# Hybrid encoder trunk on one core: rms factors spread by a matrix product of ones with a diagonal, negated logits, and half-swapping copies on ScalarE

## The chip, the core and the metric

The program runs on one NeuronCore of a Trainium2 chip. The core has TensorE (PE in the profile; its weight loads are PEld), VectorE (DVE), ScalarE (ACT), GpSimd (POOL) and SyncE (SP, which here only issues DMAs). The metric is the device time of one execution in microseconds (us); lower is better.

## What is computed

The input x is 512 tokens by 1024 features in float32. Two layers follow each other, each with an RMS norm, one input projection whose columns feed three groups, and one output projection that is added to x. The reference, cut down:

```python
def rmsnorm(x, w):
    y = x * rsqrt(mean(x * x, axis=-1, keepdims=True) + EPS)
    return y * w

def hybrid_layer(x, ...):                       # called twice
    h = rmsnorm(x, norm_w)
    aq, ak, av, ag, bq, bk, bv, bg, cu, cg = split(h @ w_in)
    # A: 4 heads, two softmax maps each, logits = q.k / 8 + bias[q - k]
    o_a = rmsnorm((softmax(l0) - lam * softmax(l1)) @ v) * silu(ag)
    # B: 4 heads of two-way retention, rotary q and k, chunks of 128
    o_b = headnorm(forward + backward) * silu(bg)
    # C: pooling over windows of 2, 4, 8, 16, minus the token, then a linear map
    o_c = pool_mix(cu) * silu(cg)
    return x + concat(o_a, o_b, o_c) @ w_out

out = rmsnorm(layer1(layer0(x)), final_norm_w)
```

## The kernel before

**Precision.** Every matrix product works on operands that are split in a high and a low part of type float32r. `split` does it: ScalarE writes the high part (a CAST), VectorE subtracts it from the source and writes the low part. `mm3` then issues three matmuls where the mathematics has one.

**Weights.** They come in 95 blocks of 512 KB and two half blocks, called granules. Each is loaded by a DMA into `wraw` (2 buffers), split by ScalarE into `wh` and by VectorE into `wl` (5 buffers each). A `wraw` buffer is free again when both have read it, so VectorE's subtraction decides when the next load may be issued.

**The order.** The kernel is first recorded as a list of operations. `Recorder.schedule` plays the five engines forward with a table of costs (`cost`, `LATENCY`) and priorities (`HIGH`) and takes at each step the operation that can start first. What comes out is a fixed order for each engine; every engine then executes its own list strictly in that order. All DMAs are issued by SP, in one list: a DMA that waits holds up all DMAs behind it. The strings in `ORDERS` say in which order the units of a layer (projections, heads, pooling groups) are recorded.

**The first layer's start.** `first_values` multiplies the transposed x by the weights before the RMS factors are known, with the norm weights alone applied. The factor of each token (1/rms) comes later, from `square` on ScalarE and a power on GpSimd, and stands in four columns `rc` (128 partitions by 4, inside the tile `edge`). The values use it per partition. All other projections of the first layer have tokens along the free axis, so there the factor is needed as a tile `rb`, 128 partitions by 512, each partition holding all 512 factors. The unit `R` of the string `START` makes it by two DMAs, through a row in DRAM:

```python
row = nc.tile("dram", "row", [S], 4, F32)
nc.sync.dma_start(row.rearrange("(t p) -> p t", t=NT), self.rc)
nc.sync.dma_start(self.rb, row.partition_broadcast(P))
```

The users of `rb` are the rotary tables `cos` and `sin` (multiplied by it once), `scaled_T` and `c_pool`.

**Half-swapping copies.** `stack_halves` lays the queries and keys of two maps or heads into partitions 0 to 63 and 64 to 127. For the keys (`dup` is true) high and low part are also copied to the other half of the partitions, 64 by 1024 elements each time, 24 times in all. `b_qk` does the same with the retention states `sx`, 64 by 512 elements, 8 times. Both are VectorE copies before (`DUP = nc.vector`); the trace calls them CAST, since the output type is float32r; `sx` lives in a tile named `T`.

**Softmax.** In `a_head` one VectorE instruction (CUSTOM_DVE_ANT_0 in the trace) adds the bias to the logits and takes each row's maximum into the tile `sm`; a second one, 128 by 1, turns the sign; ScalarE then computes the exponential with that as its bias. This happens 64 times.

Of the kernel before, what the change touches and what calls it, by code (L numbers as in the profile page):

```python
# [369 lines left out]
def record(ins: dict, out: bass.AP):  # L370
# [3 lines left out]
    def sb(tag, shape, bufs=1, dt=F32, name=None):  # L374
        return nc.tile("sb", tag, shape, bufs, dt)
# [16 lines left out]
    def soft():  # L392
        return sb("soft", [P, S], 4)
# [20 lines left out]
    nc.vector.memset(neghalf, -0.5)  # L414
    nc.scalar.copy(sb("st", [P, 4], 4), neghalf)
    ident = sb("ident", [P, P])


    granules = [(i, shape) for i, (_, _, _, shape) in enumerate(weight_granules())]
# [19 lines left out]
    def take(n):  # L439
# [2 lines left out]
        while len(wt) < min(i + WBUFS, len(granules)):  # L442
            emit_granule()
        return wt[i:i + n]

    DUP = nc.vector


    def split(dh, dl, src):
# [68 lines left out]
    def stack_halves(dst, slots, src, scale, dup):  # L518


        for m in range(2):
            a, b = slice(64 * m, 64 * m + 64), slice(64 - 64 * m, P - 64 * m)
            s0 = slots + (2 * m if dup else m)
            hi = dst[a, s0, :]
            lo = dst[a, s0 + 1, :] if dup else dst[b, s0, :]
            if scale == 1.0:
                split(hi, lo, src[a, :])
            else:
                nc.scalar.activation(hi, src[a, :], AF.Copy, scale=scale)
                nc.vector.scalar_tensor_tensor(lo, src[a, :], scale, hi.bitcast(F32), op0=ALU.mult, op1=ALU.subtract)  # L530
            if dup:
                DUP.tensor_copy(dst[b, s0:s0 + 2, :], dst[a, s0:s0 + 2, :].bitcast(F32))

    def headnorm(ov, scale, g):

# [96 lines left out]
    def bias_tables():  # L632

        oh, ohr = ttile(), ttile(dt=F32R)
        rb = soft()[0:32, 0:4]
        rbs = sb("rbs", [64, 4], 1, F32R)
        nc.sync.dma_start(rb, ins["rel_bias"])
        nc.sync.dma_start(oh[0:64, :], ins["c_onehot"])
        nc.scalar.copy(ohr[0:64, :], oh[0:64, :])
        split(rbs[0:32, :], rbs[32:64, :], rb)  # L640
        gsb = ttile()
        for i in range(2):
            ps = lgp()
            nc.tensor.matmul(ps[0:4, :], rbs, ohr[0:64, HALF[i]], start=True, stop=True)
            nc.vector.tensor_copy(gsb[0:4, HALF[i]], ps[0:4, :])
        nc.sync.dma_start(gdram, gsb[0:4, :])


        dl = soft()
        nc.sync.dma_start(dl, ins["diff_lambda"].rearrange("l a d -> (l a d)").partition_broadcast(P))  # L650
        dv = dl.rearrange("p (l a b d) -> p l a b d", l=2, a=2, b=2)
        pr = soft()[:, 0:256].rearrange("p (l a d) -> p l a d", l=2, a=2)
        nc.vector.tensor_tensor(pr, dv[:, :, :, 0, :], dv[:, :, :, 1, :], op=ALU.mult)
        ls = cols[:, 12:16]
        nc.vector.tensor_reduce(ls, pr.rearrange("p l a d -> p (l a) d"), axis=AX.X, op=ALU.add)
        nc.scalar.activation(ls, ls, AF.Exp)
        for l in range(DEPTH):
            lam_init = 0.8 - 0.6 * math.exp(-0.3 * l)
            nc.vector.tensor_tensor(lam_t[l], ls[:, 2 * l:2 * l + 1], ls[:, 2 * l + 1:2 * l + 2], op=ALU.subtract)
            nc.vector.tensor_scalar(lam_t[l], lam_t[l], lam_init, None, op0=ALU.add)  # L660
# [18 lines left out]
    class Layer:  # L679
# [18 lines left out]
        def first_values(self):  # L698

            self.vh, self.vl = sb("vh", [P, NT, 512], 1, F32R), sb("vl", [P, NT, 512], 1, F32R)  # L700
            self.rb, self.rc = sb("rb", [P, S]), edge[:, 28:32]

            dummy = sb("soft", [P, S], 4, mybir.dt.bfloat16)
            nc.vector.memset(dummy, 0.0)
            warm = tpp()
            for _ in range(WARM):
                nc.tensor.matmul(warm[:, 0:256], dummy[:, 0:P], dummy[:, 0:256], start=True, stop=True)
            banks = [lgp(), lgp(), ovp(), pj()]
            for u in START.split():
                i = int(u[1:] or 0)  # L710
                if u[0] == "k":
                    xw = ttile()
                    nc.sync.dma_start(xw[:, 0:S + 4], ins["xT_w"][i * P:(i + 1) * P, :])
                    raw, w = xw[:, 0:S], xw[:, S:S + 1]
                    nc.scalar.activation(self.hh[:, i, :], raw, AF.Copy, scale=w)
                    nc.vector.scalar_tensor_tensor(self.hl[:, i, :], raw, w, self.hh[:, i, :].bitcast(F32), op0=ALU.mult, op1=ALU.subtract)
                    if i % 2 == 0:
                        emit_granule(2 if i < FINE else 1)
                    wh, wl = wt[i // 2]
                    for t in range(NT):  # L720
                        ts = slice(t * P, (t + 1) * P)
                        mm3(banks[t], self.hh[:, i, ts], self.hl[:, i, ts], wh[:, i % 2, :], wl[:, i % 2, :], i == 0, i == KD - 1)
                elif u[0] == "x":
                    load_x(i)
                    for half in range(2):
                        square(i, half, soft())
                    nc.vector.tensor_copy(self.rc[:, i:i + 1], stats[i][:, 2:3])
                elif u[0] == "I":
                    nc.sync.dma_start(ident, ins["c_ident"])
                elif u[0] == "R":  # L730
                    row = nc.tile("dram", "row", [S], 4, F32)
                    nc.sync.dma_start(row.rearrange("(t p) -> p t", t=NT), self.rc)
                    nc.sync.dma_start(self.rb, row.partition_broadcast(P))
                else:
                    for t in range(NT):
                        self.store_values(t, banks[t])
            wstate[0] = 4
# [51 lines left out]
        def b_qk(self, pr):  # L789
# [30 lines left out]
            for hd in range(2):  # L820
                a, b = slice(64 * hd, 64 * hd + 64), slice(64 - 64 * hd, P - 64 * hd)
                src = sv[a, :, hd * P:(hd + 1) * P]
                nc.scalar.activation(sx[a, hd, 0, :, :], src, AF.Copy, scale=0.125)
                nc.vector.scalar_tensor_tensor(sx[a, hd, 1, :, :], src, 0.125, sx[a, hd, 0, :, :].bitcast(F32),
                                               op0=ALU.mult, op1=ALU.subtract)
                nc.vector.tensor_copy(sx[b, hd, :, :, :], sx[a, hd, :, :, :].bitcast(F32))
            self.qk["B", pr] = t, qx, sx

        def b_head(self, h):
# [24 lines left out]

        def a_qk(self, h):
            t = sb("qk", [P, 6, S], 2, F32R)
            stack_halves(t, 0, *self.scaled_T(proj_T(self.hh, self.hl), 0.125), False)
            stack_halves(t, 2, *self.scaled_T(proj_T(self.hh, self.hl)), True)
            self.qk["A", h] = t

        def a_head(self, h):
# [3 lines left out]
            for half in range(2):  # L865
                ah, al = ttile([P, NT, 256], F32R), ttile([P, NT, 256], F32R)
                for i2 in range(2):
                    i = half * 2 + i2
                    st = sb("sm", [P, 8], 4)
                    e = []  # L870
                    for mp in range(2):
                        lg = lgp()
                        mm_stacked(lg, qk, mp, slice(i * P, (i + 1) * P))
                        s = soft()
                        nc.vector.tensor_tensor_reduce(s, lg, toep_tile(bt, i), scale=1.0, scalar=-3e38,
                                                       op0=ALU.add, op1=ALU.max, accum_out=st[:, mp:mp + 1])
                        nc.vector.tensor_scalar(st[:, 2 + mp:3 + mp], st[:, mp:mp + 1], -1.0, None, op0=ALU.mult)
                        nc.scalar.activation(s, s, AF.Exp, bias=st[:, 2 + mp:3 + mp], accum_out=st[:, 4 + mp:5 + mp])
                        e.append(s)
                    nc.vector.reciprocal(st[:, 6:8], st[:, 4:6])  # L880
                    nc.vector.tensor_tensor(st[:, 7:8], st[:, 7:8], lam_t[self.l], op=ALU.mult)
                    nc.scalar.activation(e[1], e[1], AF.Copy, scale=st[:, 7:8])
                    nc.vector.scalar_tensor_tensor(e[0], e[0], st[:, 6:7], e[1], op0=ALU.mult, op1=ALU.subtract)
                    tv = transpose4(e[0])
                    split(ah[:, :, i2 * P:(i2 + 1) * P], al[:, :, i2 * P:(i2 + 1) * P], tv)
                for kt in range(NT):
                    mm3(ov[:, half * 256:(half + 1) * 256], self.vh[:, kt, h * P:(h + 1) * P],
                        self.vl[:, kt, h * P:(h + 1) * P], ah[:, kt, :], al[:, kt, :], kt == 0, kt == NT - 1)
# [226 lines left out]
```

## Time and profile before

| what | value |
|---|---|
| median of 3 runs | 682.93 us (681.54 to 682.99) |
| the profiled execution, own time | 682.16 us |
| its span, first to last instruction | 680.4 us |
| PE busy | 660.3 us (97%) |
| DVE busy | 500.3 us (74%) |
| ACT busy | 354.0 us (52%) |
| POOL busy | 30.3 us (4%) |
[...]

The profile shows one execution. Busy time of PE is modelled: a 128x512 matmul is shown with some 0.40 us, while the next one starts 0.23 us after it, so they overlap, and lost time of PE is better read from the starts. A wait that is shown for an engine costs something only where that engine, or who waits for it, is the one that sets the end.

### The profile page before, as it was taken

What the parts mean: (1) busy time and instruction counts of PE and PEld (TensorE: products, weight loads), DVE (VectorE), ACT (ScalarE), POOL (GpSimd) and SP (SyncE); (2) the same over time, 40 slices, a digit from 0 to 9 for tenths busy, and PEclk for the clock granted to TensorE, in tenths of its full rate; (3) what the DMA queues carried; (4) which work ended last, traced back from release to release, by engine and by line L of the source; (5) the groups of instructions that cost most, each with busy time, mean ns of one, the idle gap of its engine ahead of it and who ended that gap; (6) DMA issues with size and microseconds to landing.
All of it is one profiled execution on the core that took longest, in us unless ns stands there. A gap on an engine that the chain in (4) does not pass through costs nothing. (4 is left out here: it accounts for less than half of the span.)

```text
span 680.4 us, 8912 instructions
## 1 busy us (share of the span) xinstructions
PE 660.3 (97%) x3171; PEld 541.3 (80%) x3171; DVE 500.3 (74%) x954; ACT 354.0 (52%) x701; POOL 30.3 (4%) x51
## 2 busy tenths in 40 slices
PE   9959999999999999999999999899999999999996
PEld 6747887888788888887888888688888887888785
DVE  4558988787787998976574778767568857887733
ACT  6524683534376866553443766344437765665321
POOL 0000000000000000001010000000000000000011
PEclk9969999999999999999999999999999999999999
DMA  8436434422225223243312423532331143124302
GB/s 309 163 123 187 141 93 125 124 93 78 87 61 171 77 91 104 72 116 95 107 63 78 139 68 85 139 109 73 104 118 59 62 137 107 61 92 97 92 31 93
DMA packets 29973, 71.86 MB, mean 106 GB/s; under 512 B 6004, under 2 KB 10260, under 8 KB 29928
## 3 DMA queue, kind: packets, MB, share of 16 engines
q1 hardware_dynamic: 29928, 71.29, 34.4%
q8 instruction: 25, 0.41, 0.3%
q14 instruction: 20, 0.16, 0.1%
HBM read 69.09 MB, written 2.18 MB: 105 GB/s over the span
## 5 line engine op out<-in xcount | busy, mean ns | idle before, releaser
L1047 PE MATMUL pj<-hh,wh 128*128 128x512 f32 x448 | 178.5, 400 | 8.7 <-ACT wh L1047 7.2
L1047 PE MATMUL pj<-hl,wh 128*128 128x512 f32 x448 | 177.8, 397 | 0.0
L1047 PE MATMUL pj<-hh,wl 128*128 128x512 f32 x448 | 177.2, 397 | 0.0
L1047 ACT CAST wh<-wraw 128x1024 fp32r<-128x1024 f32 (+1 forms) x97 | 100.8, 1039 | 108.5 <-PE pj L1047 73.9
L1047 DVE TENSOR_TENSOR wl<-wraw,wh 128x1024 fp32r<-128x1024 f32 (+1 forms) x97 | 117.3, 1209 | 28.5 <-ACT wh L1047 28.0
L1047 PEld LDWEIGHTS pj<-hh,wh 128*128 128x128 f32 x448 | 84.9, 190 | 27.8 <-ACT wh L1047 7.6
L1047 PEld LDWEIGHTS pj<-hh,wl 128*128 128x128 f32 x448 | 84.8, 189 | 18.7
L1047 PEld LDWEIGHTS pj<-hl,wh 128*128 128x128 f32 x448 | 84.8, 189 | 17.8
L1047 PE MATMUL pj<-wh,mAC 128*128 128x512 f32 (+1 forms) x264 | 87.9, 392 | 0.4 <-ACT mAC L1047 0.2
L1047 ACT ACTIVATE soft<-soft,sm 128x512 f32<-128x512 f32 x96 | 67.8, 718 | 33.7 <-DVE sm L1047 33.2
L1047 DVE TENSOR_TENSOR x<-x,pj 128x512 f32<-128x512 f32 (+1 forms) x65 | 43.5, 675 | 23.3 <-PE pj L1047 22.7
L1047 PEld LDWEIGHTS pj<-wh,mAC 128*128 128x128 f32 x264 | 48.9, 188 | 11.4 <-ACT mAC L1047 0.6
L1047 PE MATMUL lg<-qk 128*128 128x512 f32 (+1 forms) x192 | 51.3, 361 | 1.6 <-DVE soft L1047 1.6
L1047 PE MATMUL pj<-wl,mAC 128*128 128x512 f32 (+1 forms) x132 | 51.4, 389 | 0.0
L1047 POOL TENSOR_TENSOR st<-st,neghalf 128x4 f32<-128x4 f32 (+1 forms) x28 | 25.1, 897 | 477.4 <-DVE st L1047 379.3
L1047 DVE CUSTOM_DVE_ANT_0 soft<-lg,wide 128x512 f32<-128x512 f32 x64 | 43.2, 685 | 2.0 <-PE tp L1047 0.4
L1047 PE MATMUL pj<-wh,mB 128*128 128x512 f32 (+1 forms) x136 | 44.5, 383 | 0.0
L1047 PE MATMUL pj<-wh,hl 128*128 128x512 f32 x104 | 41.4, 398 | 0.0
L1047 PE MATMUL pj<-wh,hh 128*128 128x512 f32 x104 | 41.3, 397 | 0.0
L1047 PE MATMUL pj<-wl,hh 128*128 128x512 f32 x104 | 41.2, 396 | 0.0
L1047 PEld LDWEIGHTS lg<-qk 128*128 128x128 f32 x192 | 32.5, 188 | 9.6 <-DVE soft L1047 2.6
L1047 PE MATMUL ov<-T,vh 128*128 128x256 f32 x192 | 39.1, 283 | 0.4 <-DVE og L1047 0.3
(151 smaller groups left out, 948.7 us busy)
## 6 DMA issues: line engine op xcount, KB each, us to landing
wraw<-in_wg SPq DMA_DIRECT2D x95, 512.0 KB, 3.9
hn<-row SPq DMA_DIRECT2D x16, 256.0 KB, 3.9
wide<-gd SPq DMA_DIRECT2D x8, 448.0 KB, 3.8
T<-in_xT_w SPq DMA_DIRECT2D x8, 258.0 KB, 4.6
x<-in_x SPq DMA_DIRECT2D x8, 256.0 KB, 4.8
wide<-dd SPq DMA_DIRECT2D x8, 256.0 KB, 4.8
out<-T SPq DMA_DIRECT2D x8, 256.0 KB, 2.1
qd<-dd SPq DMA_DIRECT2D x8, 128.0 KB
```

The costliest lines, as they stand in the source:

```text
L1047: op.inst = getattr(getattr(tc.nc, name), method)(*[real(a) for a in op.args], **{k: real(v) for k, v in op.kw.items()})
```

## The change

Four things are altered.

1. **The factors' tile.** The two DMAs of unit `R` go. VectorE multiplies the identity matrix by each of the four columns of `rc` (a diagonal in each 128 by 128 block of `dg`), `split` makes `dh` and `dl` of it, and two matmuls with a stationary matrix of ones (128 by 128, exact in float32r) add up each column over the partitions. The sum, the factor of that column's token, arrives in all 128 partitions of a PSUM bank; ScalarE copies it to `rb`. The ones are made at the program's start, in the buffers of the tiles `T` and `u`.
2. **Negated logits.** The queries are scaled by -0.125, the bias table is written with its sign turned, the custom instruction takes the minimum, and the exponential runs with `scale=-1.0`. The instruction that turned the sign, 64 times, goes.
3. **Keys' copies** of `stack_halves` run on ScalarE.
4. **States' copies** of `b_qk` run on ScalarE.

```diff
@@ record @@
     ident = sb("ident", [P, P])
+    ones = sb("u", [P, UW], 1, F32R)[:, 0:P]
+    onesf = sb("T", [P, 1024], 4)[:, 0:P]
+    nc.vector.memset(onesf, 1.0)
+    nc.vector.tensor_copy(ones, onesf)
...
-    DUP = nc.vector
...
@@ stack_halves @@
             if dup:
-                DUP.tensor_copy(dst[b, s0:s0 + 2, :], dst[a, s0:s0 + 2, :].bitcast(F32))
+                nc.scalar.copy(dst[b, s0:s0 + 2, :], dst[a, s0:s0 + 2, :].bitcast(F32))
...
@@ bias_tables @@
-            nc.vector.tensor_copy(gsb[0:4, HALF[i]], ps[0:4, :])
+            nc.vector.tensor_scalar(gsb[0:4, HALF[i]], ps[0:4, :], -1.0, None, op0=ALU.mult)
...
@@ first_values, unit R @@
-                    row = nc.tile("dram", "row", [S], 4, F32)
-                    nc.sync.dma_start(row.rearrange("(t p) -> p t", t=NT), self.rc)
-                    nc.sync.dma_start(self.rb, row.partition_broadcast(P))
+                    dg, dh, dl = soft(), sb("soft", [P, S], 4, F32R), sb("soft", [P, S], 4, F32R)
+                    for t in range(NT):
+                        nc.vector.tensor_scalar(dg[:, t * P:(t + 1) * P], ident, self.rc[:, t:t + 1], None, op0=ALU.mult)
+                    split(dh, dl, dg)
+                    ps = tpp()
+                    nc.tensor.matmul(ps, ones, dh, start=True, stop=False)
+                    nc.tensor.matmul(ps, ones, dl, start=False, stop=True)
+                    nc.scalar.copy(self.rb, ps)
...
@@ b_qk @@
-                nc.vector.tensor_copy(sx[b, hd, :, :, :], sx[a, hd, :, :, :].bitcast(F32))
+                nc.scalar.copy(sx[b, hd, :, :, :], sx[a, hd, :, :, :].bitcast(F32))
...
@@ a_qk @@
-            stack_halves(t, 0, *self.scaled_T(proj_T(self.hh, self.hl), 0.125), False)
+            stack_halves(t, 0, *self.scaled_T(proj_T(self.hh, self.hl), -0.125), False)
...
@@ a_head @@
-                        nc.vector.tensor_tensor_reduce(s, lg, toep_tile(bt, i), scale=1.0, scalar=-3e38,
-                                                       op0=ALU.add, op1=ALU.max, accum_out=st[:, mp:mp + 1])
-                        nc.vector.tensor_scalar(st[:, 2 + mp:3 + mp], st[:, mp:mp + 1], -1.0, None, op0=ALU.mult)
-                        nc.scalar.activation(s, s, AF.Exp, bias=st[:, 2 + mp:3 + mp], accum_out=st[:, 4 + mp:5 + mp])
+                        nc.vector.tensor_tensor_reduce(s, lg, toep_tile(bt, i), scale=1.0, scalar=3e38,
+                                                       op0=ALU.add, op1=ALU.min, accum_out=st[:, mp:mp + 1])
+                        nc.scalar.activation(s, s, AF.Exp, bias=st[:, mp:mp + 1], scale=-1.0, accum_out=st[:, 4 + mp:5 + mp])
```

Since the planner plays all engines forward, the order of the whole program is made anew. At three places it matters for what follows. A row names the line, the operation, what it writes and reads with the buffers' numbers, and the shape; numbers differ between the two programs.

SP's list of DMAs before, from the last two x tiles on (`row` and `rb` are the two DMAs of unit `R`; `wraw` are weight granules):

```order
L1047 DMA x_0_253<-in_x 128x512
L1047 DMA wraw_262<-in_wg 128x1024
L1047 DMA wraw_276<-in_wg 128x1024
L1047 DMA soft_287<-in_decay 8x2
L1047 DMA row_319<-edge_112 128x4x1
L1047 DMA rb_339<-row_319 128x512
L1047 DMA wraw_348<-in_wg 128x1024
L1047 DMA wraw_397<-in_wg 128x1024
```

And SP's list at the same place now:

```order
L1055 DMA x_0_254<-in_x 128x512
L1055 DMA wraw_263<-in_wg 128x1024
L1055 DMA wraw_277<-in_wg 128x1024
L1055 DMA soft_312<-in_decay 8x2
L1055 DMA wraw_345<-in_wg 128x1024
L1055 DMA wraw_413<-in_wg 128x1024
L1055 DMA wraw_423<-in_wg 128x1024
```

The two DMAs are gone, and the load of the next granule (`wraw_348` before, `wraw_345` now) stands directly behind the small load of the decays.

ACT's list before, from the cast of the first gate's weights on (`vh` are the values, `wh` the weights' high parts; `wh_381` is the granule that `wraw_348` above loads):

```order
L1047 CAST wh_315<-wraw_262 128x1024
L1047 ACTIVATE vh_325<-lg_119,edge_112 128x512
L1047 ACTIVATE vh_325<-lg_121,edge_112 128x512
L1047 ACTIVATE vh_325<-ov_125,edge_112 128x512
L1047 ACTIVATE soft_287<-soft_287 8x2
L1047 ACTIVATE vh_325<-pj_128,edge_112 128x512
L1047 CAST wh_356<-wraw_276 128x1024
L1047 CAST wh_381<-wraw_348 128x1024
```

And now (`soft_329` is `dh`, `rb_377` the factors' tile out of the PSUM bank `tp_342`; `wh_387` answers to `wh_381`):

```order
L1055 CAST wh_320<-wraw_263 128x1024
L1055 CAST soft_329<-soft_289 128x512
L1055 ACTIVATE vh_335<-lg_120,edge_113 128x512
L1055 ACTIVATE vh_335<-lg_122,edge_113 128x512
L1055 ACTIVATE soft_312<-soft_312 8x2
L1055 ACTIVATE vh_335<-ov_126,edge_113 128x512
L1055 ACTIVATE vh_335<-pj_129,edge_113 128x512
L1055 CAST wh_365<-wraw_277 128x1024
L1055 COPY rb_377<-tp_342 128x512
L1055 CAST wh_387<-wraw_345 128x1024
```

Two instructions are new, the cast of `dh` ahead of the values and the copy of `rb` between two weight casts; the other eight stand in the order of before.

PE's list before, from the last matmuls of the values on (`pj_337` is the projection of the first gate):

```order
L1047 MATMUL pj_128<-wl_266,hh_104 128x512
L1047 MATMUL pj_128<-wh_257,hl_110 128x512
L1047 MATMUL pj_337<-hh_104,wh_315 128x512
L1047 MATMUL pj_337<-hl_110,wh_315 128x512
L1047 MATMUL pj_337<-hh_104,wl_327 128x512
```

And now:

```order
L1055 MATMUL pj_129<-wl_267,hh_105 128x512
L1055 MATMUL pj_129<-wh_258,hl_111 128x512
L1055 MATMUL tp_342<-soft_329,u_75 128x512
L1055 MATMUL pj_348<-hh_105,wh_320 128x512
L1055 MATMUL pj_348<-hl_111,wh_320 128x512
L1055 MATMUL pj_348<-hh_105,wl_331 128x512
L1055 MATMUL pj_348<-hh_105,wh_320 128x512
L1055 MATMUL pj_348<-hl_111,wh_320 128x512
L1055 MATMUL tp_342<-soft_350,u_75 128x512
L1055 MATMUL pj_348<-hh_105,wl_331 128x512
```

The two products with the ones (`u_75`) are set ahead of and between the first gate's matmuls (`pj_348`), which followed the values directly before.

## Rows read from the trace of the kernel before

**Rows 1.** The page: busy times, and TensorE's granted clock in 40 slices.

```profile
PE 660.3 (97%) x3171; PEld 541.3 (80%) x3171; DVE 500.3 (74%) x954; ACT 354.0 (52%) x701; POOL 30.3 (4%) x51
...
PEclk9969999999999999999999999999999999999999
```

**Rows 2.** Waits of PE: who waited for whom, us in total, times, longest.

```profile
PE pj L1047 <- ACT wh L1047: 7.2, 1, 7.2
PE lg L1047 <- DVE soft L1047: 1.6, 2, 1.3
PE pj L1047 <- DVE gate L1047: 1.5, 1, 1.5
PE tp L1047 <- DVE soft L1047: 1.2, 1, 1.2
PE lg L1047 <- ACT T L1047: 1.0, 1, 1.0
```

**Rows 3.** Timeline of PE, 27 to 47 us: start, duration, instruction, idle before.

```profile
27.88 0.40 PE L1047 MATMUL pj<-hh,wh 128*128 128x512 f32 x1
...
33.71 0.39 PE L1047 MATMUL pj<-hl,wh 128*128 128x512 f32 x1
41.32 0.80 PE L1047 MATMUL pj<-hh,wh 128*128 128x512 f32 x1 [7.22 <-ACT wh L1047]
...
46.56 0.40 PE L1047 MATMUL pj<-hh,wh 128*128 128x512 f32 x1
```

**Rows 4.** One window: stretch, its length, busy of five engines, PEclk, DMA share, GB/s.

```profile
41.32:46.56 5.24, 5.24 (x12) 4.17 (x13) 4.86 (x20) 1.68 (x2) 0.00 (x0) 0.51 0.64 191
```

**Rows 5.** Timelines of ACT, SP and DVE around that wait.

```profile
40.22 1.04 ACT L1047 CAST wh<-wraw 128x1024 fp32r<-128x1024 f32 x1 [10.52 <-DMA wraw<-in_wg]
...
25.06 0.39 SPq L1047 DMA_DIRECT2D row<-edge  x1
35.30 0.34 SPq L1047 DMA_DIRECT2D rb<-row  x1
35.74 7.45 SPq L1047 DMA_DIRECT2D wraw<-in_wg  x3
...
25.50 1.23 DVE L1047 TENSOR_TENSOR wl<-wraw,wh 128x1024 fp32r<-128x1024 f32 x1 [0.47 <-ACT wh L1047]
...
39.07 0.69 DVE L1047 TENSOR_TENSOR cos<-cos,rb 128x512 f32<-128x512 f32 x1 [8.56 <-DMA rb<-row]
...
41.63 1.21 DVE L1047 TENSOR_TENSOR wl<-wraw,wh 128x1024 fp32r<-128x1024 f32 x1
```

**Rows 6.** Timelines of ACT and DVE: what the new steps stand beside.

```profile
28.07 0.69 ACT L1047 ACTIVATE vh<-pj,edge 128x512 fp32r<-128x512 f32 x1
28.66 1.04 ACT L1047 CAST wh<-wraw 128x1024 fp32r<-128x1024 f32 x1
...
55.78 1.05 ACT L1047 ACTIVATE T<-T 8x1024 f32<-8x1024 f32 x1
...
0.89 0.27 DVE L1047 MEMSET soft<- 128x256 uint32 x1
```

**Rows 7.** Groups of instructions by shape: count, busy us, mean ns, idle before.

```profile
L1047 DVE CAST qk<-qk 64x1024 fp32r<-64x1024 f32 x24 | 16.5, 689 | 0.7
L1047 DVE TENSOR_SCALAR sm<-sm 128x1 f32<-128x1 f32 x64 | 8.7, 146 | 0.0
L1047 DVE CAST T<-T 64x512 fp32r<-64x512 f32 x8 | 3.4, 422 | 0.3
...
L1047 ACT CAST qk<-soft 64x512 fp32r<-64x512 f32 x32 | 19.8, 618 | 7.4 <-DVE soft L1047 3.5 <-PE lg L1047 3.4
L1047 ACT COPY hn<-ov 128x512 f32<-128x512 f32 x16 | 9.4, 586 | 16.1 <-DVE og L1047 11.0 <-PE ov L1047 4.0 <-DVE mAC L1047 0.9
...
L1047 ACT CAST T<-T 64x1024 fp32r<-64x1024 f32 x1 | 1.1, 1054 | 0.2 <-PE ov L1047 0.2
```

**Rows 8.** One window (columns as in rows 4), where retention heads are prepared.

```profile
70.00:80.00 10.00, 10.00 (x46) 8.07 (x45) 8.71 (x12) 7.90 (x12) 0.00 (x0) 1.00 0.40 136
```

## The prediction

> **What bounds the kernel now.** I read the busy times first, then PE's waits, then the timelines around the longest wait. PE is busy for 660.3 of 680.4 us, DVE for 500.3 and ACT for 354.0 [rows 1]. So PE sets the end, and work on DVE or ACT costs time only where PE waits for it. PE's list of waits [rows 2] has one large entry: 7.2 us, once, on a weight cast of ACT. The next ones are 1.6 us and less.
>
> That wait begins at 34.1 us and ends at 41.32 [rows 3]. [...] The whole loss comes from starts of matmuls. From 27.88 to 33.71 there are 25 steps, (33.71 - 27.88) / 25 = 0.233 us each. From 33.71 to 46.56 there are 13 steps (the one across the wait, and twelve behind it), which at that pace need 3.03 us; they took 12.85. The loss is **9.82 us**: some 7.4 of idleness and 2.4 of half clock.
>
> The cause stands in the rows of the other engines [rows 5]. The awaited cast began at 40.22, having waited for its granule. SP issued that load at 35.74, right behind `rb<-row`, issued at 35.30, which had to wait for `row<-edge`, issued at 25.06. The write of 512 single numbers to DRAM took 10 us, and SP's list stood still for it. DVE stood still as well: `cos` times `rb` began at 39.07 after 8.56 us of idleness, and the subtractions that make `wl` are queued behind it. Would SP have been free, the load could have been issued when its buffer was: a subtraction on the earlier granule began at 25.50 and took 1.23, so at 26.8.
>
> **The change part by part.**
>
> *The DMAs of unit R.* Both go; the load of the next granule moves up behind a small load. What must then be in time?
> - Issue 26.8, plus the landing as it was seen (35.74 to 40.22, 4.48 us [rows 5]): 31.3. Cast 1.04: 32.3.
> - PE ends the values at 27.88, has two products more (0.47) and the first gate's 24 matmuls (5.59): 33.94. It wants that cast two matmuls later, at 34.4. Reserve 2.1 us.
>
> *What takes their place.* Four multiplications of 128x128 on DVE: between 0.146 (128x1) and 0.422 (64x512) each [rows 7]; I take 0.2. They stand where DVE idled, ahead of the subtraction at 25.50. Cast of `dh`: 0.62 (the cast of 512 elements a partition [rows 7]). Subtraction for `dl`: 0.69 (as `cos` [rows 5]), from 26.73 on, so done by some 27.8 with three tiny steps between; PE wants it after the sixth matmul, at 29.3. The copy of `rb`: ACT's last values cast was at 28.07 [rows 6]; the `dh` cast moves it to 28.7, it takes 0.69, a weight cast 1.04, the copy 0.59 [rows 7]: `rb` is there at 31.0 instead of 39.07. On the path stand only the two products: **+0.47 us**.
>
> *DVE behind rb.* From `cos` to the beginning of the second subtraction it took 41.63 - 39.07 = 2.56 us [rows 5]; one values' low part (0.7, the size of `cos`) now stands between. So the first `wl` is ready at 31.0 + 2.56 + 0.7 = 34.3; PE wants it after four matmuls, at 34.87. Reserve 0.6 us: tight, and taken as no wait. Behind it 48 matmuls run until 45.1.
>
> *The next tight place* is the decay tables' exponential on ACT, behind a chain of small steps on DVE; the cast of a later granule is queued behind it. From `cos` to the end of the exponential it took 56.83 - 39.07 = 17.8 us [rows 5, 6]. From 31.0 that gives 48.8, and 49.8 with the cast; PE wants that cast 16 matmuls behind 45.1, at 48.8. So the bound from above is a wait of 1.0 us. From below it is none, since in the trace of before this chain was also held by PE itself, which now is earlier. I take none and keep 1.0 for the range.
>
> *The half clock.* With no long idleness there, nothing in the trace gives it a reason: in all other slices the digit is 9, with PE at work [rows 1]. Those 2.4 us go too.
>
> *The start.* A memset of 128x128 stands ahead of the memset on which PE's first matmuls wait: half of a 128x256 one, 0.27 / 2 = 0.14 [rows 6]. Between 0 (PE's first real matmul waits for a DMA) and 0.14; I take **0.1**.
>
> *Copies to ACT.* DVE loses 24 x 0.689 and 8 x 0.422, 19.9 us. ACT gains 24 x 1.054 and 8 x 0.618, 30.2 us [rows 7]. Where they lie, ACT is busy 7.9 and DVE 8.7 of 10 us [rows 8]; a pair of heads moves two copies of each kind, so 3.3 us more for ACT and 2.2 less for DVE, spread over some 20 us. ACT has the room. Cost on the path: bounded from above by all of ACT's surplus, 10.3 us (the slower rival), from below by a gain, since waits of 1.6, 1.5 and 1.2 us are ended by DVE [rows 2]. I take **0**: the keys' cast itself ends none of the listed waits.
>
> [...] ACT needs 1054 ns for 64x1024 where DVE needs 689 [rows 7], 365 ns more a copy. [...]
>
> *The sign.* 64 instructions of 146 ns, 9.3 us with the time counted singly, 8.7 as busy time [rows 7], each between a maximum and its exponential. PE has other matmuls to run in the attention heads, so on the path **0**; from below a part of the DVE waits above.
>
> **Sum.** -9.82 + 0.47 + 0.1 = -9.25 us. Against the profiled execution (682.16 us, 680.4 of them span) this gives 672.9; that execution lies 0.77 below the median of 682.93, so for the median **673.7 us**.
>
> **The rivals.**
> - *As summed:* 673.7; with the small terms' bounds 671.9 to 675.5.
> - *The wait comes back in part.* `rb` or the decay chain is 1.5 us later than reckoned: PE then waits 0.9 at the first tight place and, counting both, 2.5 at the second. 673.7 + 2.5 = 676.2. For it: the reserves of 0.6 and -1.0. Against: PE's own wait is contained in the 17.8 us.
> - *More is won.* The lighter DVE ends the waits that it caused: 1.6 + 1.5 + 1.2 = 4.3 [rows 2]; two thirds of them, 2.9, give 670.8. Against: the waits on banks and on attention weights can hang on a DMA or on the new order as well.
> - *The wait was hidden anyway.* If the granule's load is late for another reason (its landing takes twice the 4.48 us in the traffic there), the cast ends at 36.8 instead of 32.3, PE waits 2.4, and its clock might fall again (2.4): 678.5. Against: the 4.48 us were seen with the load of `rb` right ahead [rows 5], which is gone.
> - *Slower.* ACT works strictly in order, so a copy of 1.05 us holds up what is queued behind it, the values and the casts for PE. If all 32 copies pass on their surplus of 10.3 us to PE, the sum is -9.25 + 10.3 = +1.0: 684.0. It turns at 9.25 / 32 = 0.29 us of PE for each copy; to be slower by over 0.2% it takes 0.33. Against: ACT is idle for half of the span [rows 1].
> - *The change doesn't do what it says:* excluded here as far as the order goes; the two DMAs are gone and the load has moved up.
>
> **How the numbers follow.** Chances: as summed 0.66, back in part 0.13, more won 0.12, hidden anyway 0.05, slower 0.04. A measurement of this kernel can tell about 0.2% (1.4 us) from no change. Faster by more: all but the last, less 0.01 that several small losses meet: 0.95. Within: 0.02. Slower: 0.03. The range of 8 in 10 takes the first case whole and the nearer parts of the second and third: 670.9 to 676.8.
>
> **What would show it.** Right: no wait of PE over 1 us between 28 and 60 us, `wraw` issued near 27 us, `rb` copied near 31, the clock digit of the third slice at 9. DVE some 27 us less busy, ACT some 31 more. Wrong: PE waits on `wl` near 34.9 or on a `wh` cast near 49; ACT's copies among the instructions that end waits of PE in the heads; or new waits of several us in the second layer, where only the order has changed.

## The result, and the profile after

The changed kernel takes 672.37 us in the median of 4 runs (671.47 to 673.67), where the kernel before took 682.83 (681.54 to 682.99). The ratio is 0.9852, 95% interval 0.9829 to 0.9876, which is 8.5 to 11.7 us less; the forecast was 9.25 less, 673.7. The profiled execution of after took 673.67 us, 671.9 of them span. It is the slowest of its four, so the two profiles lie 8.49 us apart and not 10.46.

Busy times, clock digits and PE's complete list of waits, for after (for before [rows 1, 2]):

```profile
PE 658.4 (98%) x3173; PEld 539.2 (80%) x3173; DVE 478.6 (71%) x865; ACT 385.5 (57%) x735; POOL 30.1 (4%) x51
...
PEclk9999999999999999999999999999999999999999
```

```profile
PE tp L1055 <- DVE soft L1055: 2.2, 2, 1.4
PE pj L1055 <- DVE gate L1055: 1.4, 1, 1.4
PE lg L1055 <- DVE soft L1055: 1.2, 2, 0.8
PE tp L1055 <- ACT hn L1055: 1.1, 2, 0.9
PE pj L1055 <- ACT soft L1055: 0.6, 1, 0.6
PE pj L1055 <- DVE vl L1055: 0.5, 1, 0.5
PE pj L1055 <- ACT u L1055: 0.2, 1, 0.2
```

The wait of 7.2 us on the weight cast is gone, and the 6 in the clock digits with it. What remains are single waits of 1.4 us and less, none of them between 28 and 60 us. The timelines of ACT, SP, DVE and PE at the place of the old wait (start, duration, instruction, idle before):

```profile
25.47 0.63 ACT L1055 CAST soft<-soft 128x512 fp32r<-128x512 f32 x1
...
29.50 0.58 ACT L1055 COPY rb<-tp 128x512 f32<-128x512 f32 x1
29.99 1.05 ACT L1055 CAST wh<-wraw 128x1024 fp32r<-128x1024 f32 x1
...
44.75 1.06 ACT L1055 ACTIVATE T<-T 8x1024 f32<-8x1024 f32 x1 [2.11 <-DVE T L1055]
45.72 1.03 ACT L1055 CAST wh<-wraw 128x1024 fp32r<-128x1024 f32 x1
```

```profile
26.70 8.27 SPq L1055 DMA_DIRECT2D wraw<-in_wg  x3
```

```profile
30.12 0.69 DVE L1055 TENSOR_TENSOR cos<-cos,rb 128x512 f32<-128x512 f32 x1 [0.35 <-ACT rb L1055]
...
32.20 1.21 DVE L1055 TENSOR_TENSOR wl<-wraw,wh 128x1024 fp32r<-128x1024 f32 x1
```

```profile
27.69 0.39 PE L1055 MATMUL tp<-soft,u 128*128 128x512 f32 x1
27.93 0.39 PE L1055 MATMUL pj<-hh,wh 128*128 128x512 f32 x1
29.07 0.39 PE L1055 MATMUL tp<-soft,u 128*128 128x512 f32 x1
...
33.96 0.39 PE L1055 MATMUL pj<-hl,wh 128*128 128x512 f32 x1
...
36.96 0.40 PE L1055 MATMUL pj<-hh,wh 128*128 128x512 f32 x1
```

The load that was issued at 35.74 [rows 5] is now issued at 26.70, its cast begins at 29.99, and `cos` at 30.12 instead of 39.07. From 27.69 (the first product with the ones, right behind the values) to 36.96 PE makes 40 steps in 9.27 us, 0.232 us each, with nothing lost. The matmul at 36.96 is the one that stood at 46.56 [rows 3], the same number of steps behind the values: 9.6 us earlier. The other 1.1 us to 8.49 were lost again later. Behind that matmul PE is idle for 6.07 us in all, where it was 5.41 before, so 0.7 of them lie in small waits, at other places than in the trace of before; where the rest lies is not shown.

### The profile page after: what moved, and what is told of

Same layout as the page of the kernel before. It is cut to its first block, busy times and chain, and to the rows that moved or that the text cites. A ratio compares the mean times of both kernels' runs of the same rounds, so it can differ in the third digit from the quotient of the medians.

```text
span 671.9 us, 8866 instructions
## 1 busy us (share of the span) xinstructions
PE 658.4 (98%) x3173; PEld 539.2 (80%) x3173; DVE 478.6 (71%) x865; ACT 385.5 (57%) x735; POOL 30.1 (4%) x51
## 5 line engine op out<-in xcount | busy, mean ns | idle before, releaser
L1055 DVE TENSOR_TENSOR wl<-wraw,wh 128x1024 fp32r<-128x1024 f32 (+1 forms) x97 | 117.3, 1209 | 33.4 <-ACT wh L1055 32.9
```

The lines of the kernel that those rows point to most:

```text
L1055: op.inst = getattr(getattr(tc.nc, name), method)(*[real(a) for a in op.args], **{k: real(v) for k, v in op.kw.items()})
```

## The experiments

Twelve kernels were run. "Before" and "after" are the two kernels of this document; a ratio is against before.

### Which part of the change: factors alone, all but the factors

Edit of the first: before with the hunks `record` (the line `DUP` stays) and `first_values` alone. Edit of the second: after without the four lines that make the ones, and with

```diff
-                    dg, dh, dl = soft(), sb("soft", [P, S], 4, F32R), sb("soft", [P, S], 4, F32R)
...
-                    nc.scalar.copy(self.rb, ps)
+                    row = nc.tile("dram", "row", [S], 4, F32)
+                    nc.sync.dma_start(row.rearrange("(t p) -> p t", t=NT), self.rc)
+                    nc.sync.dma_start(self.rb, row.partition_broadcast(P))
```

> The kernel before with the factors' tile alone changed (ones times diagonal in place of the two DMAs); copies and sign as before. Theory (the gain is PE's one long wait and its half clock): about 9.3 us less than before, 673.5, no wait of PE over 1 us between 28 and 60 us. Rival (the gain comes from VectorE's lighter load, by copies and sign): 2 to 5 us less, 678 to 681.

> The changed kernel with the two DMAs of the factors' tile put back; copies on ScalarE and negated logits stay. Theory: within 1.5 us of before, 681.3 to 684.3, with the wait of 7 us and the half clock behind it still there. Rival (lighter VectorE): 4 us less or more, 679 and below.

Measured: factors alone 672.84 us, ratio 0.9853 (0.9837 to 0.9868). All but the factors 683.07, ratio 1.0011 (0.9991 to 1.0031), with PE's wait on `wh` there again, 7.9 us. So the factors' tile gives the whole gain, and copies and sign together nothing that can be measured.

### Copies and sign, each by itself

Edits: before with the hunks `stack_halves` and `b_qk` alone; before with the negated logits alone; after with the copies back on VectorE; and after with each moved copy done twice:

```diff
+                nc.scalar.copy(dst[b, s0:s0 + 2, :], dst[a, s0:s0 + 2, :].bitcast(F32))
                 nc.scalar.copy(dst[b, s0:s0 + 2, :], dst[a, s0:s0 + 2, :].bitcast(F32))
...
+                nc.scalar.copy(sx[b, hd, :, :, :], sx[a, hd, :, :, :].bitcast(F32))
                 nc.scalar.copy(sx[b, hd, :, :, :], sx[a, hd, :, :, :].bitcast(F32))
```

> The kernel before with only the keys' and states' copies moved to ScalarE; factors and sign as before. Theory (neither engine ends a wait that matters there; PE is the bound): DVE some 20 us less busy, ACT some 30 more, time within 1.5 us of before: 681 to 684. Rival slower: each copy holds up what is queued behind it on ScalarE and its surplus of 10.3 us is passed on to PE: 688 to 693. Rival faster: DVE's waits (4.3 us of PE) go with the lighter DVE: 678 to 680.

> The kernel before with only the logits negated: 64 sign instructions of 146 ns gone from DVE, factors and copies as before. Theory: they lie between a maximum and its exponential, but PE has other matmuls to run there, so the time is that of before within 1.5 us: 681 to 684. Rival: part of the 9.3 us lies on the path of the attention heads, and the time is 677 to 680.

> The changed kernel with the keys' and states' copies back on VectorE (so factors and sign stay changed). Theory: DVE some 20 us busier, ACT some 30 less, time that of the changed kernel within 1.5 us: 671 to 674. Rival: the copies on ScalarE cost something that another part gives back, or help: outside of that.

> The changed kernel with each of the 32 moved copies done twice on ScalarE (the second one writes the same values): some 30 us more of ACT. It measures how much room ACT has at those places. Theory: the room is there, under 2 us over the changed kernel: 672 to 674.5. Rival (what the slower case rests on: a copy holds up what is queued behind it for PE, so its time is passed on): 0.3 us and more for each copy, 10 us or more: 682 and more.

| kernel | median us | ratio, interval | DVE busy | ACT busy |
|---|---|---|---|---|
| copies only | 682.0 | 0.9977 (0.996 to 0.9994) | 481.9 | 384.0 |
| sign only | 681.41 | 0.9989 (0.9977 to 1.0001) | 495.8 | 354.6 |
| after, copies back | 671.75 | 0.9843 (0.9814 to 0.9871) | 498.3 | 355.9 |
| after, copies twice | 672.59 | 0.9856 (0.9819 to 0.9893) | 478.6 | 413.8 |

All four medians lie where the theory had them. By the ratios the copies alone are worth 1.6 us (0.4 to 2.7) and the sign alone 0.8 (-0.1 to 1.6), but neither adds to the factors' gain: after without the moved copies takes no longer than after. Doubling the copies makes ACT 28.3 us busier and leaves the time where it was. The busy line and PE's complete list of waits in that kernel:

```profile
PE 659.2 (98%) x3173; PEld 539.1 (80%) x3173; DVE 478.6 (71%) x865; ACT 413.8 (62%) x767; POOL 30.1 (4%) x51
```

```profile
PE lg L1057 <- DVE soft L1057: 2.6, 2, 1.6
PE tp L1057 <- DVE soft L1057: 1.4, 1, 1.4
PE pj L1057 <- ACT mAC L1057: 0.9, 1, 0.9
PE pj L1057 <- ACT soft L1057: 0.3, 1, 0.3
PE lg L1057 <- ACT qk L1057: 0.2, 1, 0.2
```

Only the last row is a wait on a moved copy, 0.2 us once. ACT is idle for 38% of the span even then.

### Were the standing lists the cause? Two ways round the wait

The first edit keeps both DMAs on SP and tells the planner how long the write really takes; it then sets three granule loads ahead of `rb<-row` in SP's list and two more subtractions ahead of `cos` in DVE's:

```diff
-                op.end = bus + 908
+                op.end = bus + 908 + 8200 * (isinstance(op.args[0], View) and op.args[0].base.tag == "row" and op.args[1].base.tag == "edge")
```

The second issues the two DMAs from GpSimd, so that SP's list is free, while `cos` keeps its place (a cost for the new kind of instruction was added to `cost`):

```diff
-                    nc.sync.dma_start(row.rearrange("(t p) -> p t", t=NT), self.rc)
-                    nc.sync.dma_start(self.rb, row.partition_broadcast(P))
+                    nc.gpsimd.dma_start(row.rearrange("(t p) -> p t", t=NT), self.rc)
+                    nc.gpsimd.dma_start(self.rb, row.partition_broadcast(P))
```

> The kernel before, with one number of the planner altered: the write of the 512 single factors to DRAM is reckoned 8.2 us longer. The same instructions, but rb's load now stands behind three weight loads in SP's list, and cos behind two more subtractions in VectorE's. Theory (what costs is that SP and VectorE stand still in order, not that the factors are late): the wait goes without any new instruction, 9 to 10 us less than before, 673 to 674. Rival (the factors' lateness itself holds PE, since three PSUM banks fill up): PE waits near 39 us instead, 678 or more.

> The kernel before with the two DMAs of the factors' tile issued by GpSimd, which has nothing else to do there; VectorE's order around cos is that of before. SP is free, so the next granule is issued near 27 us. Theory (VectorE's standing still at cos is a cause of its own): PE still waits some 6 to 7 us, now on a subtraction of VectorE near 34.5 us, and its clock falls: 681 to 685. Rival (SP's blocked list was the whole cause): 673 to 675.

Measured: 680.87 us, ratio 0.9967 (0.9951 to 0.9982), for the first, and 682.3, ratio 0.9998 (0.9984 to 1.0012), for the second. The first expectation was missed: neither list waited for the write any more, and yet by the medians the time fell by 1.6 us only. The second time lies where its theory had it, but not for its reason alone, as the rows below show. Timelines of SP, ACT and PE in the first kernel:

```profile
25.30 0.40 SPq L1047 DMA_DIRECT2D row<-edge  x1
27.00 13.23 SPq L1047 DMA_DIRECT2D wraw<-in_wg  x3
```

```profile
37.56 1.05 ACT L1047 CAST wh<-wraw 128x1024 fp32r<-128x1024 f32 x1 [8.05 <-DMA wraw<-in_wg]
```

```profile
39.92 0.51 PE L1047 MATMUL pj<-hh,wl 128*128 128x512 f32 x1 [0.47 <-DVE wl L1047]
...
49.46 0.47 PE L1047 MATMUL pj<-hh,wh 128*128 128x512 f32 x1 [4.16 <-DVE soft L1047]
```

And of ACT and PE in the second:

```profile
37.92 1.05 ACT L1049 CAST wh<-wraw 128x1024 fp32r<-128x1024 f32 x1 [8.32 <-DMA wraw<-in_wg]
```

```profile
39.01 0.64 PE L1049 MATMUL pj<-hh,wh 128*128 128x512 f32 x1 [5.03 <-ACT wh L1049]
...
42.68 0.79 PE L1049 MATMUL pj<-hh,wl 128*128 128x512 f32 x1 [2.59 <-DVE wl L1049]
```

In the first kernel the granule's load was issued at 27.00, and its cast could begin only at 37.56, 10.6 us later; in after the same load was followed by its cast within 3.3 us. PE itself lost only 0.5 us to that, at 39.92, since DVE had made the granule before it ready and PE had its matmuls to do. What kept the gain away is the rival of the expectation, some ten microseconds later than it was put: the factors were late. `rb<-row` was issued at 40.32, `cos`, now queued behind the late subtractions, began at 45.11, and PE waited 4.2 us at 49 us for what depends on `rb`. In the second kernel SP was free, the load was issued at 26.98, and its cast began at 37.92. PE waited 5.0 us for that cast and only then 2.6 us for a subtraction behind `cos`; the theory had the subtraction alone. So with the write in place a free list brought the cast forward by 2 to 3 us only, from 40.22 [rows 5] to 37.56 and 37.92: a load issued behind the write is slow, even if the write came from another engine's list. That was in none of my theories.

### What the write does to a load behind it

Edit: after, with the write put back and read by nobody, so that no list waits for it.

```diff
+                    row = nc.tile("dram", "row", [S], 4, F32)
+                    nc.sync.dma_start(row.rearrange("(t p) -> p t", t=NT), self.rc)
                     dg, dh, dl = soft(), sb("soft", [P, S], 4, F32R), sb("soft", [P, S], 4, F32R)
```

> The changed kernel with the write of 512 four-byte pieces put back into SP's list at its old place, and read by nobody: rb is still made by the product of ones with the diagonal, so neither SP nor VectorE waits for the write. Theory (the write also holds the DMA engines, so the granule's load issued behind it lands late, as it did 10.5 us after issue in the run with the longer reckoned write): the load is issued near 27 us and lands at 36 to 38, its cast ends near 38 to 39, PE wants it at 34.4 and waits 3.5 to 5 us: 676 to 679 us, with up to 2.4 us more if the clock falls. Rival (what was lost was only the standing of the two lists, SP's and VectorE's): the load lands 3 to 5 us after issue and the time is that of the changed kernel, 672 to 673.5.

Measured: 681.29 us (678.91 to 683.27), ratio 0.9972 (0.9948 to 0.9995): a write that nobody reads takes back about four fifths of the gain. That is more than the theory's 676 to 679, and within the 2.4 us that it added in case the clock falls, which it did. Timelines of SP, ACT and PE:

```profile
25.78 0.39 SPq L1057 DMA_DIRECT2D row<-edge  x1
27.39 13.75 SPq L1057 DMA_DIRECT2D wraw<-in_wg  x3
```

```profile
30.01 0.57 ACT L1057 COPY rb<-tp 128x512 f32<-128x512 f32 x1
38.48 1.04 ACT L1057 CAST wh<-wraw 128x1024 fp32r<-128x1024 f32 x1 [7.91 <-DMA wraw<-in_wg]
```

```profile
39.58 0.80 PE L1057 MATMUL pj<-hh,wh 128*128 128x512 f32 x1 [5.08 <-ACT wh L1057]
```

And its windows (columns as in rows 4), with the stretch behind the wait last:

```profile
27.00:29.00 2.00, 2.00 (x11) 1.62 (x10) 2.00 (x9) 2.00 (x5) 0.00 (x0) 1.00 2.45 66
29.00:31.00 2.00, 2.00 (x10) 1.65 (x9) 1.85 (x6) 1.58 (x3) 0.14 (x2) 1.00 0.05 4
31.00:33.00 2.00, 2.00 (x11) 1.59 (x10) 2.00 (x7) 0.00 (x0) 0.00 (x0) 1.00 0.98 45
33.00:35.00 2.00, 1.50 (x7) 0.89 (x5) 0.98 (x2) 0.00 (x0) 0.00 (x0) 1.00 0.57 25
35.00:37.00 2.00, 0.00 (x0) 0.00 (x0) 0.00 (x0) 0.00 (x0) 0.00 (x0) 1.00 0.26 39
37.00:39.00 2.00, 0.00 (x0) 0.00 (x0) 0.00 (x0) 0.52 (x1) 0.00 (x0) 0.55 0.85 332
...
39.58:44.82 5.24, 5.24 (x14) 4.15 (x15) 4.86 (x18) 2.44 (x3) 0.00 (x0) 0.57 0.30 100
```

`rb` was there at 30.6 and the load issued in time, and PE still waited 5.1 us. The last two columns show why: for eight microseconds from 29 us on the engines begin 4 to 45 GB/s, and what is left of this load and of the next one (issued at 33.98) comes at 332 GB/s in the last window. In after the window 27 to 29 alone has 211 GB/s, at a share of 0.56. Bytes and shares stand in the window in which a packet begins, so a share above 1 (2.45) means that packets begun there lasted beyond it. In before, where SP issued no load behind the write, they begin nothing at all between 27 and 35 us, and yet SP had to wait for the write's end until 35.30 [rows 5]. So it is not bandwidth that the write takes:

```profile
27.00:29.00 2.00, 2.00 (x10) 1.65 (x9) 1.45 (x4) 2.00 (x5) 0.00 (x0) 1.00 0.00 0
...
33.00:35.00 2.00, 1.10 (x5) 0.56 (x3) 0.00 (x0) 0.00 (x0) 0.00 (x0) 1.00 0.00 0
```

In the stretch behind the wait of the kernel with the unread write 14 matmuls start in 5.24 us at a granted clock of 0.57; at 0.233 us a step there would be 22.5, so (22.5 - 14) x 0.233 = 2.0 us go to the lower clock. With the 5.1 of idleness PE loses some 7.1 us here, against 9.82 in before.

The load was reported after the write both times: here the write landed 11.0 us after issue, at 36.8, and the load 11.1 us after its own, at 38.5; when GpSimd had issued the write, `rb<-row`, which waited for it, was issued at 35.74, and the load's cast began at 37.92. Whether a load's report has to wait for the write's is not shown; the windows show that the bytes themselves came late.

### Number or size of the pieces

Three more edits. Before, with the row as 128 pieces of 16 bytes (the DMAs and the waits stay; the factors then stand in the row in another order, so most tokens get another one's, and the outputs are not those of the layers):

```diff
-                    nc.sync.dma_start(row.rearrange("(t p) -> p t", t=NT), self.rc)
+                    nc.sync.dma_start(row.rearrange("(p t) -> p t", t=NT), self.rc)
```

After, with unread writes of 512 pieces of 16 bytes (four DMAs of 128 pieces each), and with one of 256 pieces of 4 bytes:

```diff
+                    row = nc.tile("dram", "row", [4 * S], 4, F32)
+                    for t in range(NT):
+                        nc.sync.dma_start(row[t * S:(t + 1) * S].rearrange("(p j) -> p j", j=NT), self.rc)
```

```diff
+                    row = nc.tile("dram", "row", [S], 4, F32)
+                    nc.sync.dma_start(row[0:2 * P].rearrange("(t p) -> p t", t=2), self.rc[:, 0:2])
```

> The kernel before, with one edit: the factors are written to the DRAM row as 128 pieces of 16 bytes (four factors of one partition side by side) in place of 512 pieces of 4. The factors then belong to the wrong tokens, which the time does not care for; nothing else changes, and both DMAs stay. Theory (the number of pieces is what makes the write slow): in the trace of before the other writes of 16-byte pieces land 2.0 us after issue, so the row lands near 28 us instead of 35.3, rb near 32, the granule's load near 32 to 33, and PE waits under 1 us there: 673 to 676 us. Rival (the trip through DRAM is slow, in however many pieces): the row lands after 33 us and the time is 679 or more.

> The changed kernel with an unread write at the place of the old one, as in the run with the unread write of 512 four-byte pieces, but with 512 pieces of 16 bytes: the four factors of each partition, written by four DMAs to four stretches of a longer row. It tells the number of pieces from their size. If the number decides: the granule's load behind it lands 9 to 11 us after issue, PE waits some 5 us, 678 to 682 us. If it is the size of 4 bytes: the write lands in some 2 to 3 us, the load about 4 us after issue, 671.5 to 674 us. I lean to the size (0.6): 128 pieces of 16 bytes landed 2.3 us after issue, so four times as many should need at most 4 times the packets' time and not the long rest behind them.

> The changed kernel with an unread write of half the size at the place of the old one: two of the four columns of factors, 256 pieces of 4 bytes. If the price goes with the number of four-byte pieces (10.5 us for 512, so some 20 ns each): the write lands some 5 us after issue, the granule's load near 31 to 33 us, in time or up to 1 us late for PE, 672 to 674 us. If a fixed delay comes with any such write: the load lands near 37 us as with 512 pieces, 679 to 682 us.

| write | landing (issue to reported end) | cast behind the load began | PE's wait there | median us, ratio |
|---|---|---|---|---|
| 128 x 16 B, read | 2.3 us, by `rb`'s issue | 32.34 | none | 673.85, 0.9865 (0.9851 to 0.988) |
| 512 x 16 B, unread | 3.1 us, median of the four DMAs | 31.62 | none | 674.96, 0.989 (0.9846 to 0.9933) |
| 256 x 4 B, unread | 10.6 us | 36.88 | 3.1 us | 679.88, 0.9969 (0.9942 to 0.9995) |
| 512 x 4 B, unread | 11.0 us | 38.48 | 5.1 us | 681.29, 0.9972 (0.9948 to 0.9995) |

The landings stand in the lists of DMA issues (KB each, median us from issue to landing), the first of the kernel with 512 pieces of 16 bytes, the second of that with 256 of 4, the third of that with 512 of 4:

```profile
row<-edge SPq DMA_DIRECT2D x4, 2.0 KB, 3.1
```

```profile
row<-edge SPq DMA_DIRECT2D x1, 1.0 KB, 10.6
```

```profile
row<-edge SPq DMA_DIRECT2D x1, 2.0 KB, 11.0
```

The casts behind the load with 512 pieces of 16 bytes and with 256 of 4, and, of the kernel with the row in 128 pieces, the issue of `rb<-row` and `cos`:

```profile
31.62 1.05 ACT L1058 CAST wh<-wraw 128x1024 fp32r<-128x1024 f32 x1 [1.33 <-DMA wraw<-in_wg]
```

```profile
36.88 1.04 ACT L1057 CAST wh<-wraw 128x1024 fp32r<-128x1024 f32 x1 [6.22 <-DMA wraw<-in_wg]
```

```profile
27.32 0.33 SPq L1047 DMA_DIRECT2D rb<-row  x1
```

```profile
31.19 0.69 DVE L1047 TENSOR_TENSOR cos<-cos,rb 128x512 f32<-128x512 f32 x1 [0.69 <-DMA rb<-row]
```

It is not the number of pieces in all: as many pieces of 16 bytes land in 3.1 us for each of their four DMAs (the last piece began 4.0 us after the first issue), and half as many of 4 bytes need nearly as long as all. So the theory of the first of these runs, the number, does not hold, though its time came out. Of the two cases of the last expectation the fixed delay came, and not a price by the piece: some 10 us with either number. The size of 4 bytes fits all four rows, but one other difference goes with it: every DMA of 16-byte pieces had 128 of them, one from each partition, and those of 4-byte pieces took two or four from each. A single DMA of 128 pieces of 4 bytes was not tried, so the two are not told apart. With 512 pieces of 16 bytes the time of two runs, 674.47 and 675.46, lies somewhat above the 671.5 to 674 expected. With the row in 128 pieces nearly all of the gain is had with both DMAs left in place, since then neither the lists nor the load wait long: SP issued `rb<-row` at 27.32 and `cos` began at 31.19. What it costs besides to bring that row into the right order is not shown.

## Why the prediction came out right, step by step

**The loss.** 9.82 us by starts of matmuls, less 0.47 for two products, makes 9.35; by the same matmul 9.6 were regained, 0.2 of them by values that ended earlier. The size was right.

**The cause was incomplete.** I named SP's standing list and DVE's. The runs show a third thing, which alone is worth some 7.1 us: the write holds up the load's data (4 to 45 GB/s begun from 29 to 37 us behind the unread write). The step that a free SP would have had the load issued at 26.8 and landed 4.48 us later is therefore wrong taken by itself; with SP free and the write in place the load needed 10.6 us and more. It held only because the change removes the write as well. Where both lists were freed and the write stayed, the same working forecast 9 to 10 us; the run gave 1.6, most of the rest lost to late factors. Where SP alone was free, PE's first wait was for the load's cast, 5.0 us, which the working had in time; the run gave 0. The rival "hidden anyway" did have a late load, at 0.05, but from traffic, and not from the write.

**The new steps** were a little cheaper than reckoned. The load's landing: its cast was queued at ACT until 29.99, so 3.3 us or less, for 4.48. `rb` at 30.1 for 31.0. The first `wl` at 33.4 for 34.3, so the reserve at the tight place was larger than 0.6 us. The decay tables' exponential began at 44.75 and ended at 45.8, for the bound of 48.8: from `cos` to that end it took 15.7 us, for 17.8 in before. That fits the argument for taking no wait, that the 17.8 contained PE's own. The four diagonals took 0.28 us each in the mean instead of 0.2, hidden as the rest. Of the 0.1 us at the start nothing was left at the end of the values, which came 0.2 us earlier; why they did is not shown.

**The half clock** is seen in before in the 12 steps behind the wait: 5.24 us, where 0.233 each would make 2.80, at a granted clock of 0.51 [rows 4]. It went with the wait: granted clock 1.00 in all windows of after from 25.5 to 39 us. The unread write brought both back together, a wait of 5.1 us and a clock of 0.57 in the 5.24 us behind it.

**Copies.** 0 taken, 0 measured. ACT +31.5 us for 31. The slower rival needed 0.33 us of PE for each copy; 32 more copies cost (672.59 - 672.37) / 32 = 0.01 us each, within the scatter.

**More won** did not happen. DVE became 21.7 us lighter (for 27: the sign is worth 4.5 of busy time in its own run and not 8.7, the copies 18.4 and not 19.9), and PE's waits on DVE in after still sum to 2.2 + 1.4 + 1.2 + 0.5 = 5.3 us, for 5.0 in the complete list of before (4.3 of them in rows 2). A lighter DVE did not shorten them.

## What to carry over

A wait's price is the sum over everything that stands still behind it, and a transfer can hold up the next one in the DMA engines as well as in the list that issues it (here a load behind an unread write could be used 11.1 us after its issue instead of 3.3): ask of each slow DMA what was issued after it, from any engine. The transposing write to DRAM in pieces of 4 bytes was such a DMA here even at 1 KB (10.6 us to land); with 16 bytes side by side (2.3 us; where the reader can take that order), or with a product of ones and a diagonal for a broadcast along the free axis, the delay was gone. To find which of several standing things costs the time, put the suspected operation back with nobody waiting for it.

## What the hardware did that I had not expected

A write of 256 or 512 pieces of 4 bytes took 10.6 and 11.0 us to land, for 1 and 2 KB, where 512 pieces of 16 bytes, in four DMAs, took 3.1 each. A 512 KB load issued 1.6 us behind the larger one could be used 11.1 us after its issue instead of 3.3, and a load from SP 10.9 us after it when GpSimd had issued the write. A price by the piece is not what is seen here, as half the number took nearly the same time. Why these writes are slow and those of 16 bytes are not stays open; sizes between were not tried, nor one piece of 4 bytes from each partition.
